# Larger base blocks on VectorE for the triangular inverse of a gated-delta chunk, with their operations preferred

## The chip, the cores and the metric

The kernel runs on one core of one Trainium2 chip. The metric is the device time of one execution in microseconds; for the kernel before it is the median of three runs. The profile shows one execution of the same program, taken by the hardware profiler; its times are in us from the start of the span. Engines are TensorE (PE; PEld are its weight loads), VectorE (DVE), ScalarE (ACT), GpSimd (POOL) and SyncE (SP).

## What is computed

One inference step of a two-layer decoder for 256 prompt tokens and 8 sample tokens that share the weights. Each layer adds a mixer (four mLSTM heads and eight gated-delta heads fed by one input projection), a cross-attention and a SwiGLU block to the residual; a final norm follows. What matters here is the gated-delta rule of a prompt, shown without batch and heads, for one chunk with keys k, decays g (cumulated) and step sizes beta:

```
decay_ts = exp(g_t - g_s)  for s <= t
A        = strictly_lower(decay_ts * (k @ k.T) * beta_s)
rhs      = v - exp(g) * (k @ S)
U        = triangular_solve(I + A, rhs)          # unit lower triangular
wu       = beta * U
o        = exp(g) * (q @ S) + (q @ k.T * decay_ts) @ wu
S        = exp(g_last) * S + (exp(g_last - g) * k).T @ wu
```

The keys and queries are normalised first, which needs the sum of squares of each row. The reference cuts the 256 tokens into chunks of 64, the kernel into two chunks of 128; the result is the same sum.

## The kernel before, in words

**Streams.** Nearly all time goes into products with weights. `stream` (with `block`) brings a weight block of 512 KB by DMA on SyncE's queue, splits it into a rounded part on ScalarE (`wh`, line 55) and the rest on VectorE (`wl`, line 61), and multiplies: per block 24 matmuls of 264 columns, three for each product (tile `acc`). One stream of 256 output features over 2048 inputs is 96 matmuls. The splits and what takes the accumulators out of PSUM stand under `tc.high_priority(offset=PRIO)` with PRIO = 1000.

**TensorE's order is written out by hand; the others' is planned.** The whole program stands under a manual schedule for TensorE: its instructions run in the order in which the Python code issues them. The other engines' instructions are ordered by a planner that runs before the launch: of the instructions that are ready in its own timeline it prefers those that were issued earlier, and `high_priority(offset=n)` counts an instruction as issued n earlier.

**Chains between the streams.** Everything beside the streams is a Python generator (a chain). `mm` and `tr` advance a clock by each matmul's columns / 2.4; a chain yields a number of these units, and `pump`, called after every few stream matmuls, resumes the chains whose time has come. So `yield 13000.0` puts the next matmuls of a chain that much further back in TensorE's order, to give the other engines time. If they aren't done by then, TensorE stands. `finish` runs chains that have to be over before an output projection.

**The mixer's order in a layer.** Four pairs of gated-delta heads, g = 0 to 3: for each, the streams of q, k and v (`gdn_inputs`, with the convolutions on VectorE), then two chains are spawned, `gdn_prompt` and `gdn_sample`; the stream of the gate z of the pair before comes next. Then the mLSTM streams and chains. A pair's `gdn_prompt` starts only when the one before has formed its last state (`R.formed`).

**`gdn_prompt`, step by step** (two heads and two chunks give four 128x128 matrices, side by side in tiles of 4x128 columns):
1. TensorE transposes the keys (tile kT) and ScalarE sums their squares (line 640); VectorE scales (`kss`, `rk`, `bs`, `kw`).
2. TensorE forms the products of keys (kk); VectorE makes N of them (line 58), which is A scaled.
3. `base_blocks` inverts the diagonal blocks of BASE = 8. ScalarE gathers the 32x32 diagonal blocks into tile u; VectorE transposes (lines 612, 617, 620) and runs a back substitution column by column, two operations for each column k (a product into scratch space of tile Dt, a subtraction in u); ScalarE copies the result into Dm. Dt is the transpose of Dm.
4. Meanwhile TensorE transposes values, queries (qT, with squares on ScalarE, line 671) and N (NT, copied to A).
5. After the long pause of line 680 come the doublings, for b = 8, 16, 32, 64: a product with A (pp), on VectorE a masked copy (Pf), a product with Dt (pd), on VectorE a subtraction in Dm and a transpose (line 715). Each turns inverses of b-blocks into inverses of 2b-blocks.
6. The solution, the outputs and the states of both chunks (pu, pS, pr), and the squares of the outputs (line 772).

`gdn_sample` does the same rule for the eight sample tokens (dks, then `rank1` with the matmuls dS that update the states on VectorE). The mLSTM chains (mqk, mvT, mkT, mn, mC) use the same four PSUM buffers (tag "m") as all chains.

**Scratch for squares.** `M.junk` hands out a tile of 128x256 with one buffer (`bufs=1`) for the unused elementwise result of a sum of squares; each call is a new tile in the same buffer.

Of the kernel before, what the change touches and what calls it, by code (L numbers as in the profile page):

```python
# [27 lines left out]
MEM = 256  # L28
EPS = 1e-6
WB, VB, SB, NV = 10, 6, 7, 6  # L30
BASE = 8
PRIO = 1000
Q0, K0, V0, O0 = 0, 512, 1024, 2048
IF0 = 3072
GQ0, GK0, GV0, GZ0 = 3080, 4104, 5128, 6152
# [13 lines left out]
def kernel(ctx: ExitStack, tc: tile.TileContext, io: dict, outs: list):  # L49
# [10 lines left out]
    def tt(out, a, b, op, eng=None):  # L60
        (eng or dve).tensor_tensor(out=out, in0=a, in1=b, op=op)  # L61
# [6 lines left out]
    def mm(out, lhsT, rhs, start=True, stop=True):  # L68
        n = 1
        for x in rhs.shape[1:]:  # L70
            n *= x
        clock[0] += max(n, lhsT.shape[-1]) / 2.4 * (1 if rhs.dtype == F32R else 4)
        pe.matmul(out=out, lhsT=lhsT, rhs=rhs, start=start, stop=stop)  # L73
# [37 lines left out]
    def ps(name):  # L111
        return pm.tile([P, 512], F32, name=name, tag="m")
# [429 lines left out]
    class Mix:  # L542

        def __init__(self, mx):

            self.mx, self.sampling = mx, False

        def w(self, name, shape=(4, P)):
            return self.mx.tile([P] + list(shape), F32, name=name, tag="w", bufs=WB)

# [17 lines left out]
            return self.mx.tile([P] + list(shape), F32, name=name, tag=name, bufs=2)  # L568

        def junk(self, p=P):  # L570
            return self.mx.tile([P, DV], F32, name="junk", tag="junk", bufs=1)[:p]

    def four(t):
        return t.rearrange("p (i t) -> p i t", i=4)
# [47 lines left out]
    def gdn_prompt(l, g, s, G, M, R):  # L622
# [12 lines left out]
        pkn = ps("kT")  # L635
        for i in range(4):
            tr(pkn[:, i * P:(i + 1) * P], ch(k, i))
        kss, rk, bs, kd = M.c("kss"), M.c("rk"), M.c("bs"), M.c("kd")
        for i in range(4):
            act.activation(M.junk()[:, :P], pkn[:, i * P:(i + 1) * P], AF.Square, accum_out=kss[:, i:i + 1])  # L640
        kw = M.w("kw")
        tt(kw, four(pkn), bc(E[:, :, P - 1], 2, P), ALU.mult)
        dve.tensor_scalar(out=kss, in0=kss, scalar1=4.0 * EPS, scalar2=None, op0=ALU.add)
        dve.reciprocal(out=rk, in_=kss)
        tt(bs.rearrange("p (h c) -> p h c", c=2), rk.rearrange("p (h c) -> p h c", c=2), bcol, ALU.mult)
        dve.tensor_scalar(out=kd, in0=kss, scalar1=0.25, scalar2=None, op0=ALU.mult)
        power(kd, hp)

        pk_ = ps("kk")
        for i in range(4):  # L650
            mm(pk_[:, i * P:(i + 1) * P], ch(k, i), ch(k, i))
        N = M.w("N")
        for i in range(4):
            stt(N[:, i], pk_[:, i * P:(i + 1) * P], bs[:, i:i + 1], E[:, i], ALU.mult, ALU.mult)

        Dm, Dt = M.w("Dm"), M.w("Dt")
        pool.memset(Dm, 0.0)
        base_blocks(N, Dm, Dt, M.v("u", (2, P)))
        yield 4500.0
        pv = ps("vT")  # L660
        for i in range(4):
# [6 lines left out]
            tr(pqn[:, i * P:(i + 1) * P], ch(q, i))  # L668
        qd = M.c("qd")
        for i in range(4):  # L670
            act.activation(M.junk()[:, :P], pqn[:, i * P:(i + 1) * P], AF.Square, accum_out=qd[:, i:i + 1])
        dve.tensor_scalar(out=qd, in0=qd, scalar1=4.0 * EPS, scalar2=float(DK), op0=ALU.add, op1=ALU.mult)
        power(qd, hm)
        A = M.w("A")
# [2 lines left out]
        for i in range(4):  # L677
            tr(pa[:, i * P:(i + 1) * P], N[:, i])
        copy(A, four(pa))
        yield 13000.0  # L680
        b = BASE
        while b < P:
            def halves(t, which, i=None):
# [85 lines left out]
        R.formed = True  # L769
        oss = M.c("oss")  # L770
        for i in range(4):
            act.activation(M.junk()[:, :P], o[:, i], AF.Square, scale=qd[:, i:i + 1], accum_out=oss[:, i:i + 1])
# [15 lines left out]
    def gdn_sample(l, g, s, G, M, R, S, smp):  # L788

        h0 = 2 * g  # L790
        kv, k3, r3, kqf = smp[:4]
        while M.sampling:
            yield 500.0
        M.sampling = True
        for kind, at in ((1, 0), (0, 32), (2, 64)):
            pool.tensor_copy(out=kv[:, :, at:at + NB], in_=s[kind][:, :, T:C])
            if kind < 2:
                pool.tensor_copy(out=kqf[:, :, at:at + 41 * 7 + 1:41], in_=s[kind][:, :, T:C])
        if not G.ready:
            while not G.ready:  # L800
                yield 500.0
            yield 8000.0
        yield 10500.0
        pks = ps("dks")
        for j in range(2):
            tr(pks[:, T + j * P:T + (j + 1) * P], kv[:, j])
        for j in range(2):
            for b in range(NB):
                mm(pks[:40, j * P:(j + 1) * P], kqf[:, j, b * 40:(b + 1) * 40], S[:, j, b], b == 0, b == NB - 1)
        kn, qn, vN = M.n("dkn"), M.n("dqn"), M.n("dvn")  # L810
        for i, (d, f) in enumerate(((kn, 1.0), (qn, 1.0), (vN, 0.5))):
            copy(d, pks[32 * i:32 * i + NB, T:].rearrange("p (h t) -> p h t", h=2), scale=f)
        qk = M.c("dqk", (2, 2))[:NB]
        c = M.c("dc", (2,))[:NB]
        for j in range(2):
            act.activation(M.junk(NB)[:, :P], kn[:, j], AF.Square, accum_out=qk[:, 0, j:j + 1])
            act.activation(M.junk(NB)[:, :P], qn[:, j], AF.Square, accum_out=qk[:, 1, j:j + 1])
# [12 lines left out]
        tt(c, c, bk, ALU.mult)  # L830
        oN = qn
        for j in range(2):
            stt(vN[:, j], pks[:NB, j * P:(j + 1) * P], a1[:, j:j + 1], vN[:, j], ALU.mult, ALU.add)
            dve.tensor_scalar(out=oN[:, j], in0=pks[32:32 + NB, j * P:(j + 1) * P], scalar1=er[:, j:j + 1],
                              scalar2=None, op0=ALU.mult)
            stt(oN[:, j], vN[:, j], c[:, j:j + 1], oN[:, j], ALU.mult, ALU.add)
        tt(kn, kn, bc(bk, 2, P), ALU.mult)
        three(k3, kn, False)
        three(r3[:, :, :P], vN, True)
        yield 12000.0  # L840
        ev = G.gs[:, h0 * NB:(h0 + 2) * NB].rearrange("p (h b) -> p h b", h=2)
        for j in range(2):
            yield from rank1(S[:, j], k3[:, j], r3[:, j], ev[:, j], M.mx, P)
            nc.sync.dma_start(out=s_S[l, :, h0 + j].rearrange("b k v -> k b v"), in_=S[:, j])
        M.sampling = False
        q = M.c("dq", (2,))[:NB]
        for j in range(2):
            act.activation(M.junk(NB)[:, :P], oN[:, j], AF.Square, accum_out=q[:, j:j + 1])
        dve.tensor_scalar(out=q, in0=q, scalar1=1.0 / DK, scalar2=EPS, op0=ALU.mult, op1=ALU.add)
        power(q, hm)  # L850
        tt(oN, oN, bc(q, 2, P), ALU.mult)
        yield 2500.0
        while R.z is None:
            yield 500.0
        pb = ps("db")
        for j in range(2):
            tr(pb[:, j * NB:(j + 1) * NB], oN[:, j], NB)
        x = M.c("dx", (2, NB))
        tt(x, pb[:, :2 * NB].rearrange("p (h b) -> p h b", h=2), R.z[:, :, T:C], ALU.mult)
        for j in range(2):  # L860
            split_gain(R.hh[:, R.at + j, T:C], R.hl[:, R.at + j, T:C], x[:, j], g_gain(l, h0 + j))
# [52 lines left out]
    def mlstm_prompt(l, h, q, k, v, G, M, R, ncol):  # L914
# [39 lines left out]
        dve.reciprocal(out=rd, in_=rd)  # L954
        for c in range(2):
            dve.tensor_scalar(out=hn[:, c], in0=pn[c][:, :DV], scalar1=rd[:, c:c + 1], scalar2=None, op0=ALU.mult)
            act.activation(M.junk(), hn[:, c], AF.Square, accum_out=hss[:, c:c + 1])
# [15 lines left out]
    def mlstm_sample(l, g, q, k, vs, G, M, R, Cs, smp):  # L973
# [63 lines left out]
        three(r3, vN, True)  # L1037
        s2 = M.c("sss", (2,))[:NB]
        for j in range(2):
            act.activation(M.junk(NB), hN[:, j], AF.Square, accum_out=s2[:, j:j + 1])  # L1040
# [527 lines left out]
```

## Time and profile before

| | |
|---|---|
| median of 3 runs | 2974.95 us (2973.18 to 2977.75) |
| the profiled execution | 2973.59 us |
| its span, first to last instruction | 2971.8 us |
| busy: TensorE, VectorE, ScalarE, GpSimd | 98%, 67%, 50%, 17% of the span |
| granted TensorE clock, mean over the span | 0.995 |
| VectorE busy from 80 to 120 us | 36.06 us of 40 |
| VectorE busy from 700 to 1600 us (layer 0's SwiGLU block) | 557.58 us of 900 |

A line such as "L73 PE MATMUL pp<-Dm,A 128*128 128x64 f32" names the line of the kernel (often that of a helper), the engine, the operation, the tile written and the tiles read by the program's names, and the shape. In a timeline a start and a duration stand ahead of it, and in brackets behind it the idle time of the engine just before, with what ended it. A row of a view by stretches gives the stretch, its length, each engine's busy time with its number of instructions (TensorE, weight loads, VectorE, ScalarE, GpSimd), the granted clock, the share of the DMA engines and GB/s. A row for a tile gives shortest, median and longest duration in ns, and the first and last start.

### The profile page before, as it was taken

To read this page: it belongs to the slowest core of one execution; us is meant where nothing else is said; L and a number is where in the kernel's file an instruction comes from. 1 tells how busy PE (TensorE), PEld (TensorE's weight loads), DVE (VectorE), ACT (ScalarE), POOL (GpSimd) and SP (SyncE) were. 2 spreads that over 40 slices of the span, in tenths; PEclk is the share of its full clock that TensorE was granted. 3 is DMA by queue.
4 is the path that set the end of the run, shared out by engine and by line. 5 is a ranking of instruction groups with operands and counts; after the bars stand their busy time and mean duration, and the time that the engine had idled before them with its cause. 6 is when DMAs were issued, how large, how long until landed. Compare 5 with 4: busy or idle time off the path is not lost.

```text
span 2971.8 us, 57750 instructions
## 1 busy us (share of the span) xinstructions
PE 2905.8 (98%) x23219; PEld 2829.3 (95%) x23219; DVE 2001.9 (67%) x3443; ACT 1486.3 (50%) x2505; POOL 503.5 (17%) x662
## 2 busy tenths in 40 slices
PE   8989999999999999999999999999999999999998
PEld 7989999978999999999999899999699999999998
DVE  7978776877555555555688877678765555555555
ACT  6656555666433343333466655556654333343435
POOL 5222100352100000000142211104520000001001
PEclk9999999999999999999999999999999999999999
DMA  7655565666666666666665564757756666666664
GB/s 193 167 147 157 152 199 161 214 212 190 183 179 180 182 179 182 179 181 180 181 182 153 151 181 120 215 153 222 231 171 179 183 179 181 181 180 183 178 183 130
DMA packets 381252, 530.08 MB, mean 178 GB/s; under 512 B 25576, under 2 KB 226224, under 8 KB 380960
## 3 DMA queue, kind: packets, MB, share of 16 engines
q1 hardware_dynamic: 364328, 498.74, 57.0%
q0 software_dynamic: 7424, 25.20, 2.8%
q10 hardware_dynamic: 9232, 2.45, 0.4%
q8 instruction: 182, 2.98, 0.4%
q14 instruction: 86, 0.70, 0.1%
HBM read 502.88 MB, written 23.83 MB: 177 GB/s over the span
## 4 chain that ended last, share of the span: by engine, by line
PE 88%; DVE 6%; ACT 3%; issue 2%; DMA 1%; POOL 0%; SPq 0%; POOLq 0%; ACTq 0%; DVEq 0%
PE acc L73 77%; PE kv L73 2%; DVE wl L61 2%; DVE xl L58 1%; PE dks L73 1%; ACT wh L55 1%; PE pp L73 1%; PE pd L73 1%; DMA memn<-in_mem_prompt_dram 1%; PE dS L73 1%; DVE xT L61 0%; PE sqC L73 0%; DVE p L1363 0%; PE accg L73 0%; PE so L73 0%
## 5 line engine op out<-in xcount | busy, mean ns | idle before, releaser
L61 DVE TENSOR_TENSOR wl<-raw,wh 128x1024 fp32r<-128x1024 f32 x880 | 1092.6, 1242 | 812.1 <-ACT wh L55 810.2
L55 ACT ACTIVATE wh<-raw 128x1024 fp32r<-128x1024 f32 x880 | 930.9, 1058 | 1200.3 <-PE acc L73 1079.2
L73 PE MATMUL acc<-xh,wh 128*128 128x264 f32 x4736 | 1367.2, 289 | 6.3 <-ACT wh L55 3.5
L73 PE MATMUL acc<-xl,wh 128*128 128x264 f32 x4736 | 1349.9, 285 | 1.6 <-DVE xl L58 1.6
L73 PE MATMUL acc<-xh,wl 128*128 128x264 f32 x4736 | 1350.3, 285 | 0.5 <-DVE wl L61 0.5
L73 PEld LDWEIGHTS acc<-xh,wh 128*128 128x128 f32 x4736 | 897.1, 189 | 11.4 <-issue 5.1
L73 PEld LDWEIGHTS acc<-xl,wh 128*128 128x128 f32 x4736 | 897.8, 190 | 4.6 <-DVE xl L58 2.3
L73 PEld LDWEIGHTS acc<-xh,wl 128*128 128x128 f32 x4736 | 896.0, 189 | 1.5 <-DVE wl L61 1.4
L73 PE MATMUL acc<-ffh,wh 128*128 128x264 f32 x1408 | 400.7, 285 | 0.6 <-DVE xT L61 0.5
L73 PE MATMUL acc<-ffl,wh 128*128 128x264 f32 x1408 | 400.8, 285 | 0.0
L73 PE MATMUL acc<-ffh,wl 128*128 128x264 f32 x1408 | 400.3, 284 | 0.0
L61 POOL TENSOR_TENSOR fg<-fg,rstd 128x264 f32<-128x264 f32 x88 | 94.3, 1101 | 1306.1 <-ACT fg L1450 1286.4
L73 PEld LDWEIGHTS acc<-ffh,wh 128*128 128x128 f32 x1408 | 264.8, 188 | 1.0 <-issue 1.0
L73 PEld LDWEIGHTS acc<-ffl,wh 128*128 128x128 f32 x1408 | 265.3, 188 | 0.0
L73 PEld LDWEIGHTS acc<-ffh,wl 128*128 128x128 f32 x1408 | 265.0, 188 | 0.0
L61 DVE TENSOR_TENSOR xT<-acc,xT 128x264 f32<-128x264 f32 x512 | 190.0, 422 | 17.6 <-PE acc L73 17.0
L61 POOL TENSOR_TENSOR sa<-sa,sq 128x264 f32<-128x264 f32 x96 | 95.7, 1015 | 177.7 <-ACT sq L317 177.4
L58 DVE SCALAR_TENSOR_TENSOR xl<-xT,cst,xh 128x264 fp32r<-128x264 f32 x96 | 78.7, 857 | 0.0
L55 ACT ACTIVATE wm<-r,msk 72x128 fp32r<-72x128 f32 (+1 forms) x192 | 68.6, 425 | 18.5 <-PE dS L73 14.1
L58 DVE SCALAR_TENSOR_TENSOR y<-y,cst,y 128x255 f32<-128x255 f32 (+1 forms) x144 | 64.1, 473 | 0.8 <-ACT y L55 0.4
L55 ACT ACTIVATE xh<-xT,cst 128x264 fp32r<-128x264 f32 x80 | 39.6, 507 | 29.3 <-DVE xT L61 29.3
L61 POOL TENSOR_TENSOR vl<-vc,vh 128x512 fp32r<-128x512 f32 x32 | 44.3, 1411 | 25.7 <-ACT vh L55 25.7
(516 smaller groups left out, 3326.1 us busy)
## 6 DMA issues: line engine op xcount, KB each, us to landing
raw<-in_w_in_dram SPq DMA_DIRECT2D x224, 512.0 KB
raw<-in_ffn_w_gate_dram SPq DMA_DIRECT2D x176, 512.0 KB
raw<-in_ffn_w_up_dram SPq DMA_DIRECT2D x176, 512.0 KB
raw<-in_ffn_w_down_dram SPq DMA_DIRECT2D x176, 512.0 KB
raw<-in_w_out_dram SPq DMA_DIRECT2D x64, 512.0 KB
S<-in_state_gdn_S_dram POOLq DMA_DIRECT2D x16, 512.0 KB, 7.3
out_dram<-S SPq DMA_DIRECT2D x16, 512.0 KB
Ct<-in_state_mlstm_C_dram POOLq DMA_DIRECT2D x8, 1024.0 KB, 6.6
```

Of the source, the lines that this page charges most:

```text
L55: act.activation(out, in_, AF.Copy, scale=scale)
L58: dve.scalar_tensor_tensor(out=out, in0=a, scalar=s, in1=b, op0=o0, op1=o1)
L61: (eng or dve).tensor_tensor(out=out, in0=a, in1=b, op=op)
L73: pe.matmul(out=out, lhsT=lhsT, rhs=rhs, start=start, stop=stop)
```

## The change

BASE becomes 16: `base_blocks` inverts 16x16 blocks, with 15 columns instead of 7, and the doublings begin at b = 16, so that one of the four stages is left out. The pause ahead of the doublings grows from 13000 to 19000. From the squares of the keys to the end of `base_blocks` everything stands under `high_priority(offset=AHEAD)` with AHEAD = 600. The scratch tile for squares is made once per layer, and calls for 128 columns use its two halves in turn.

```
-BASE = 8
-PRIO = 1000
+BASE = 16
+PRIO, AHEAD = 1000, 600
...
+            self.junks, self.turn = mx.tile([P, DV], F32, name="junk", tag="junk"), 0
...
         def junk(self, p=P):
-            return self.mx.tile([P, DV], F32, name="junk", tag="junk", bufs=1)[:p]
+            self.turn = 1 - self.turn
+            return self.junks[:p], self.junks[:p, self.turn * P:(self.turn + 1) * P]
...
-        kss, rk, bs, kd = M.c("kss"), M.c("rk"), M.c("bs"), M.c("kd")
-        for i in range(4):
-            act.activation(M.junk()[:, :P], pkn[:, i * P:(i + 1) * P], AF.Square, accum_out=kss[:, i:i + 1])
...
-        Dm, Dt = M.w("Dm"), M.w("Dt")
-        pool.memset(Dm, 0.0)
-        base_blocks(N, Dm, Dt, M.v("u", (2, P)))
+        with tc.high_priority(offset=AHEAD):
+            kss, rk, bs, kd = M.c("kss"), M.c("rk"), M.c("bs"), M.c("kd")
+            for i in range(4):
+                act.activation(M.junk()[1], pkn[:, i * P:(i + 1) * P], AF.Square, accum_out=kss[:, i:i + 1])
...
+            Dm, Dt = M.w("Dm"), M.w("Dt")
+            pool.memset(Dm, 0.0)
+            base_blocks(N, Dm, Dt, M.v("u", (2, P)))
         yield 4500.0
...
         copy(A, four(pa))
-        yield 13000.0
+        yield 19000.0
```

All other sums of squares take `M.junk(...)[1]` (128 columns) or `[0]` (256 columns) instead of a new tile.

More of the change, by code (lines that the diff above doesn't have):

```diff
@@ L637, in gdn_prompt @@
             tr(pkn[:, i * P:(i + 1) * P], ch(k, i))
-        kss, rk, bs, kd = M.c("kss"), M.c("rk"), M.c("bs"), M.c("kd")
-        for i in range(4):
[L640 to L654, printed above, removed]
-        Dm, Dt = M.w("Dm"), M.w("Dt")
-        pool.memset(Dm, 0.0)
-        base_blocks(N, Dm, Dt, M.v("u", (2, P)))
+        with tc.high_priority(offset=AHEAD):
+            kss, rk, bs, kd = M.c("kss"), M.c("rk"), M.c("bs"), M.c("kd")
+            for i in range(4):
+                act.activation(M.junk()[1], pkn[:, i * P:(i + 1) * P], AF.Square, accum_out=kss[:, i:i + 1])
+            kw = M.w("kw")
+            tt(kw, four(pkn), bc(E[:, :, P - 1], 2, P), ALU.mult)
+            dve.tensor_scalar(out=kss, in0=kss, scalar1=4.0 * EPS, scalar2=None, op0=ALU.add)
+            dve.reciprocal(out=rk, in_=kss)
+            tt(bs.rearrange("p (h c) -> p h c", c=2), rk.rearrange("p (h c) -> p h c", c=2), bcol, ALU.mult)
+            dve.tensor_scalar(out=kd, in0=kss, scalar1=0.25, scalar2=None, op0=ALU.mult)
+            power(kd, hp)
+            pk_ = ps("kk")
+            for i in range(4):
+                mm(pk_[:, i * P:(i + 1) * P], ch(k, i), ch(k, i))
+            N = M.w("N")
+            for i in range(4):
+                stt(N[:, i], pk_[:, i * P:(i + 1) * P], bs[:, i:i + 1], E[:, i], ALU.mult, ALU.mult)
+            Dm, Dt = M.w("Dm"), M.w("Dt")
+            pool.memset(Dm, 0.0)
+            base_blocks(N, Dm, Dt, M.v("u", (2, P)))
         yield 4500.0
@@ L670, in gdn_prompt @@
         for i in range(4):
-            act.activation(M.junk()[:, :P], pqn[:, i * P:(i + 1) * P], AF.Square, accum_out=qd[:, i:i + 1])
+            act.activation(M.junk()[1], pqn[:, i * P:(i + 1) * P], AF.Square, accum_out=qd[:, i:i + 1])
         dve.tensor_scalar(out=qd, in0=qd, scalar1=4.0 * EPS, scalar2=float(DK), op0=ALU.add, op1=ALU.mult)
@@ L771, in gdn_prompt @@
         for i in range(4):
-            act.activation(M.junk()[:, :P], o[:, i], AF.Square, scale=qd[:, i:i + 1], accum_out=oss[:, i:i + 1])
+            act.activation(M.junk()[1], o[:, i], AF.Square, scale=qd[:, i:i + 1], accum_out=oss[:, i:i + 1])
         dve.tensor_scalar(out=oss, in0=oss, scalar1=1.0 / DK, scalar2=EPS, op0=ALU.mult, op1=ALU.add)
@@ L815, in gdn_sample @@
         for j in range(2):
-            act.activation(M.junk(NB)[:, :P], kn[:, j], AF.Square, accum_out=qk[:, 0, j:j + 1])
-            act.activation(M.junk(NB)[:, :P], qn[:, j], AF.Square, accum_out=qk[:, 1, j:j + 1])
+            act.activation(M.junk(NB)[1], kn[:, j], AF.Square, accum_out=qk[:, 0, j:j + 1])
+            act.activation(M.junk(NB)[1], qn[:, j], AF.Square, accum_out=qk[:, 1, j:j + 1])
         dve.tensor_scalar(out=qk, in0=qk, scalar1=4.0 * EPS, scalar2=None, op0=ALU.add)
@@ L847, in gdn_sample @@
         for j in range(2):
-            act.activation(M.junk(NB)[:, :P], oN[:, j], AF.Square, accum_out=q[:, j:j + 1])
+            act.activation(M.junk(NB)[1], oN[:, j], AF.Square, accum_out=q[:, j:j + 1])
         dve.tensor_scalar(out=q, in0=q, scalar1=1.0 / DK, scalar2=EPS, op0=ALU.mult, op1=ALU.add)
@@ L956, in mlstm_prompt @@
             dve.tensor_scalar(out=hn[:, c], in0=pn[c][:, :DV], scalar1=rd[:, c:c + 1], scalar2=None, op0=ALU.mult)
-            act.activation(M.junk(), hn[:, c], AF.Square, accum_out=hss[:, c:c + 1])
+            act.activation(M.junk()[0], hn[:, c], AF.Square, accum_out=hss[:, c:c + 1])
         dve.tensor_scalar(out=hss, in0=hss, scalar1=1.0 / DV, scalar2=EPS, op0=ALU.mult, op1=ALU.add)
@@ L1039, in mlstm_sample @@
         for j in range(2):
-            act.activation(M.junk(NB), hN[:, j], AF.Square, accum_out=s2[:, j:j + 1])
+            act.activation(M.junk(NB)[0], hN[:, j], AF.Square, accum_out=s2[:, j:j + 1])
         dve.tensor_scalar(out=s2, in0=s2, scalar1=1.0 / DV, scalar2=EPS, op0=ALU.mult, op1=ALU.add)
```

## The prediction

> **What bounds the kernel now.** I read the page's first and fourth parts, then TensorE's waits, then the chain of waits and the timelines around the largest of them.
>
> ```profile
> PE 2905.8 (98%) x23219; PEld 2829.3 (95%) x23219; DVE 2001.9 (67%) x3443; ACT 1486.3 (50%) x2505; POOL 503.5 (17%) x662
> ...
> PE 88%; DVE 6%; ACT 3%; issue 2%; DMA 1%; POOL 0%; SPq 0%; POOLq 0%; ACTq 0%; DVEq 0%
> ```
>
> TensorE sets the end: 98% busy, 88% of the chain that ended last. So a change pays if it takes matmuls away, or takes waits out of TensorE's order, which is written out by hand; work on VectorE costs nothing as long as TensorE doesn't come to wait for it. What TensorE waits for (columns: us in total, times, longest), without the rows of stages that the change leaves alone:
>
> ```profile
> PE pp L73 <- issue: 9.5, 2, 4.8
> ...
> PE dS L73 <- ACT junk L671: 3.4, 2, 1.7
> PE kk L73 <- DVE dqn L834: 3.4, 2, 1.7
> ...
> PE mkT L77 <- DVE N L58: 2.4, 2, 1.2
> ...
> PE mvT L77 <- DVE kw L61: 1.6, 2, 0.8
> PE NT L77 <- DVE N L58: 1.5, 3, 0.6
> ```
>
> All six lie in the inverse's chain or beside it, once per layer (NT three times). The largest, on layer 0's second pair of heads (I call the four pairs g0 to g3), in the chain of waits and then on VectorE and ScalarE:
>
> ```profile
> 193.86 5.10 PE acc L73 x42
> ...
> 203.26 4.75 issue
> 208.01 1.94 PE pp L73 x8
> 209.95 2.57 PE acc L73 x12
> ```
>
> ```profile
> 206.30 0.31 DVE L617 STREAM_TRANSPOSE u<-u 128x128 f32<-128x128 f32 x1
> ...
> 207.94 0.71 DVE L620 STREAM_TRANSPOSE Dt<-Dm 128x512 f32<-128x512 f32 x1 [1.33 <-ACT Dm L55]
> ```
>
> TensorE reached the first doubling's matmuls (pp) at 203.26, but the 8x8 blocks left VectorE only at 206.6 (L617), and their copies and transpose (L620) came after that, 2.1 us later: the "issue" is a wait for VectorE. How much of VectorE these blocks get is the question of this change. Two answers for the four base_blocks stretches of layer 0 (first transpose to the end of L617): all work first, then the instructions of tile u alone (the blocks):
>
> ```profile
> 101.20:116.20 15.00, 15.00 (x127) 14.64 (x127) 14.88 (x40) 9.88 (x26) 7.17 (x12) 1.00 0.63 177
> 187.40:206.60 19.20, 15.86 (x128) 15.41 (x126) 19.00 (x52) 10.04 (x17) 2.37 (x5) 0.97 0.76 215
> ```
>
> ```profile
> 101.20:116.20 15.00, 4.66 (x18) 0.00 (x0) 0.00 (x0) 1.00 0.63 177
> 187.40:206.60 19.20, 4.71 (x18) 0.00 (x0) 0.00 (x0) 0.97 0.76 215
> 269.60:278.40 8.80, 4.65 (x18) 0.00 (x0) 0.00 (x0) 1.00 0.28 89
> 335.30:344.60 9.30, 4.76 (x18) 0.00 (x0) 0.00 (x0) 0.83 0.21 70
> ```
>
> VectorE (third pair of columns) is full in g0 and g1, 14.88 of 15.00 and 19.00 of 19.20 us. The blocks cost 4.7 us each time, and got a share of 4.66/15.00 = 0.31, 0.245, 0.53 and 0.51.
>
> **The change part by part.** *Removed: the doubling from 8.* One instance on TensorE:
>
> ```profile
> 124.25 1.00 PE L73 MATMUL pp<-Dm,A 128*128 128x64 f32 x8
> 125.06 0.37 PE L73 MATMUL acc<-xh,wh 128*128 128x264 f32 x1
> ...
> 127.54 1.00 PE L73 MATMUL pd<-Pf,Dt 128*128 128x64 f32 x8
> 128.35 0.37 PE L73 MATMUL acc<-xh,wh 128*128 128x264 f32 x1
> ```
>
> From the first pp to the next matmul 0.81 us, from the first pd 0.81. Four pairs in two layers make eight chains: 8 x 1.62 = **-13.0 us**, all on the bounding engine, with nothing that could hide it. Two PSUM tiles per chain go too. On VectorE the masked copy, the subtraction and a transpose go, 0.42 + 0.41 + 0.70 = 1.53 us per chain:
>
> ```profile
> L61 DVE TENSOR_TENSOR Pf<-pp,up x16: 400/420/425, 126.7 to 1835.8; 128x256 f32<-128x256 f32 x16
> L61 DVE TENSOR_TENSOR Dm<-Dm,pd x40: 267/406/422, 128.6 to 1851.9; 128x256 f32<-128x256 f32 x16, 32x128 f32<-32x128 f32 x16, 64x256 f32<-64x256 f32 x8
> L715 DVE STREAM_TRANSPOSE Dt<-Dm x16: 693/702/712, 129.0 to 1838.9; 128x512 f32<-128x512 f32 x16
> ```
>
> *Added: the larger blocks.* base_blocks does two operations per column k, of 128/BASE x k elements: 14 of 16k elements before, 30 of 8k after. Their cost by size in g0, and the transposes:
>
> ```profile
> 103.08 0.27 DVE L61 TENSOR_TENSOR Dt<-u,Dt 128x112 f32<-128x112 f32 x1
> ...
> 114.77 0.18 DVE L61 TENSOR_TENSOR Dt<-u,Dt 128x16 f32<-128x16 f32 x1
> ```
>
> ```profile
> L612 DVE STREAM_TRANSPOSE Dt<-u x24: 300/570/579, 101.2 to 1806.9; 128x384 f32<-128x384 f32 x16, 128x128 f32<-128x128 f32 x8
> ```
>
> The first two rows make a line: 0.165 us plus 0.94 ns an element. The mean size is 64 elements before (16 x 4) and after (8 x 8), so each stays at 0.225 us; 30 cost 6.75 us. Five transposes of 384 columns at 0.57 (before two, and a short one at 0.30) and L617's 0.31 make 3.16: **9.9 us a chain**, against 4.7. With the 1.53 removed VectorE gets 3.7 more per chain, 29 us in all; it lies beside matmuls, and its price is only what TensorE waits at pp.
>
> *Moved: when TensorE comes for the blocks.* The pause ahead of the doublings grows from 13000 to 19000 units of the program's own matmul clock, which counts 264/2.4 = 110 for a matmul that took 5.10/42 = 0.1216 us: pp comes 6.6 us later. Due times: g0 124.25 + 6.6 = 130.9, g1 203.26 + 6.6 = 209.9, and from the first starts of pp in g2 and g3
>
> ```profile
> L73 PE MATMUL pp<-Dm,A x8: 218/275/275, 286.1 to 286.8; 128*128 128x64 f32 x8
> ```
>
> ```profile
> L73 PE MATMUL pp<-Dm,A x8: 275/275/323, 363.2 to 364.0; 128*128 128x64 f32 x8
> ```
>
> 292.7 and 369.8. A chain is 6 longer and a stage of 2100 + 1900 shorter, so each next pair starts some 2 us later in the streams; nothing waits for the last one's end.
>
> Are the blocks ready by then? At the shares of before, with 2.1 us for copies and transpose: g0 101.2 + 9.9/0.31 + 2.1 = 135.2, late; g1 187.4 + 9.9/0.245 + 2.1 = 229.9, very late; g2 269.6 + 9.9/0.53 + 2.1 = 290.4 and g3 335.3 + 9.9/0.51 + 2.1 = 356.8, in time. Once TensorE stands, no stream feeds VectorE and the rest runs nearly alone, so a wait is shorter than the lateness: in g0 29.7 x 0.31 = 9.2 us are done at the due time, and 0.7 + 2.1 = 2.8 are left; in g1 5.5 are done, 4.4 + 2.1 = 6.5 left, where 4.75 was the wait before.
>
> *Preferred: everything from the squares to the blocks*, as if written 600 instructions earlier. The weights' splits keep their 1000 and stay ahead:
>
> ```profile
> L61 DVE TENSOR_TENSOR wl<-raw,wh 128x1024 fp32r<-128x1024 f32 x880 | 1092.6, 1242 | 812.1 <-ACT wh L55 810.2
> ```
>
> One of 1.24 us for every 24 matmuls (2.92 us) takes 43%, which bounds the blocks' share at 0.57 from above; from below the old shares bound it, since the blocks were already written ahead of much that ran between their steps. I take the middle between 0.53 (VectorE with little else) and the old shares: 0.42 in g0, 0.39 in g1. g0 is then ready at 101.2 + 23.6 + 2.1 = 126.9, in time. g1 also starts earlier. Its squares on ScalarE, in the chain of waits:
>
> ```profile
> 170.78 0.50 ACT junk L772 x2
> ...
> 173.63 1.85 ACT wm L55 x6
> ...
> 178.73 0.36 ACT junk L640 x2
> ```
>
> All squares wrote one scratch tile, so those of k (L640) had to follow those of o (L772), and let other work in between, to 179.1. In two halves, and preferred, they can run from 173 to 175: 4 us earlier. Ready at 183.4 + 25.4 + 2.1 = 210.9 against 209.9: no margin at all. I take half of the old wait: **-4.7** of 9.5 us (from -9.5 to 2 x 1.75 = +3.5). The scratch tile itself costs nothing: the same ScalarE instructions. The preferred part issues no DMA; on GpSimd it puts a power of 128x4, a memset and a copy ahead, and GpSimd is busy for 17% of the span.
>
> *The clock.* TensorE's granted clock (third column from the end) fell behind these waits; I show the first, second and last of five such stretches:
>
> ```profile
> 181.40:184.80 3.40, 3.40 (x18) 3.40 (x17) 2.60 (x13) 1.35 (x7) 2.70 (x4) 0.50 0.58 167
> 205.30:212.10 6.80, 4.09 (x19) 4.12 (x20) 2.31 (x8) 1.23 (x4) 0.00 (x0) 0.50 0.74 224
> ...
> 1799.30:1802.70 3.40, 3.17 (x15) 3.17 (x16) 3.18 (x10) 2.02 (x4) 0.53 (x2) 0.51 0.02 5
> ```
>
> ```profile
> 181.23 3.72 PE acc L73 x18
> ```
>
> Behind 203.26, pp took 1.94 for 0.81 and twelve matmuls 2.57 for 12 x 0.1216: 2.2 us lost; at 181.4, eighteen took 3.72 for 2.19: 1.5 lost. g1 of layer 1 I count at 1.5 too. Half of g1's go with half of its wait, **-1.9**; the one at 181.4 hangs on the dS wait and goes, **-1.5**.
>
> The Trainium skill, "TensorE: Matmul & The Clock Gate", section "HAM oscillation", asks for no idle gap over some 3.4 us. By that rule the dS wait of 1.7 us would cost no clock, and the sum would be 1.5 us less of a gain; the row at 181.4 speaks against it.
>
> *The other waits.* NT waits for N, which is preferred now: **-1.5** (0 to -1.5). dS waits for squares of q, which follow those of k: **-2.5** of 3.4 (0 to -3.4). kk waits for a sample operation (dqn) that now stands behind preferred ones, but comes later: 0 (-3.4 to +3.4). mkT and mvT wait for g3's N and kw, sooner done but moved on into the mLSTM's use of the same four PSUM tiles: 0 (-4.0 to +4.0). What is late next is what the blocks pass: convolutions of the next pair and the state updates that free dS: **+3**, between 0 and the added 5.2 us once a layer, 10.4.
>
> **Sum:** -13.0 - 4.7 - 1.9 - 1.5 - 1.5 - 2.5 + 3 = -22.1 on the profiled execution's 2973.6 us (span 2971.8 and 1.8 around it): 2951.5. The median of the runs is 1.4 above that execution: **2953**.
>
> **The rivals.** *All in time.* The preference gets the blocks 0.5 everywhere; pp, NT, dS and kk waits go with their clock: -13.0 - 9.5 - 3.7 - 1.5 - 1.5 - 3.4 - 3.4 = -36.0, with the median's 1.4 **2939**. For it: g2 and g3 had that share. Against: 14.88 of 15.00.
>
> *The preference changes no order* (the change doesn't do what it says). For it: the blocks' operations were written before the convolutions that ran between them, and 0.31 was all they got; only their dependence on each other can explain that. Then g0 waits 2.8 + 1.5 of clock, g1 1.75 more, in both layers 12.1, against -13.0: **2974**.
>
> *VectorE has no room: slower.* The 9.9 us meet as many other operations in every pair, and the share falls to 0.3 or below in g2 as well. At 0.3: g0 1.0 + 2.1 + 1.5 = 4.6, g1 5.25 - 4.75 = 0.5, g2 23.1 x 0.3 = 6.9 done, 3.0 + 2.1 + 1.5 = 6.6; 11.7 a layer, 23.4 - 13.0 = +10.4: **2985**. It decides once new waits pass 6.5 us a layer. For it: 19.00 of 19.20; against: g2 needs only 9.9/(292.7 - 269.6 - 2.1) = 0.47, and had 0.53.
>
> **How the numbers follow.** The forecast gets 0.42, with 2943 to 2964 of its own; all in time 0.22; no order changed 0.18; no room 0.18. Faster or slower means over 0.2% (6 us), about what the runs can tell from none. Faster: 0.42 + 0.22 + 0.02 of the third; same 0.15; slower 0.18 + 0.01. The range reaches from below all in time, 2932, to 2978, and leaves out a twentieth below and the larger part of no room above.
>
> **What would show it.** 128x64 pp rows halved, and TensorE's busy time down by some 13 us: the sure step. "pp" gone from TensorE's waits: all in time; there with some 2 us per layer: the forecast; 3 us ahead of the first pp in g0: no order changed; pp waits in g2: no room. Block instructions' share of VectorE near 0.4 in the first two pairs; squares of k ended 2 us behind those of o; fewer than five half-clock stretches. Wrong in kind would be a longer wait of dS, acc or mqk in these stretches: then the blocks' preference is paid by whom they pass.

## The result, and the profile after

The changed kernel takes **2994.76 us** (median of three runs, 2990.93 to 2995.57) against 2974.95 before: a ratio of **1.0063**, 95% interval 1.0049 to 1.0077. It is slower by 19.8 us; the forecast was 2953, and the range ended at 2978.

The page of the changed kernel, its busy times and its chain of waits:

```profile
PE 2901.5 (97%) x23091; PEld 2825.9 (94%) x23091; DVE 2019.8 (67%) x3562; ACT 1479.6 (49%) x2505; POOL 507.1 (17%) x660
...
PE 84%; DVE 9%; ACT 2%; DMA 2%; issue 2%; POOL 1%; SPq 0%; POOLq 0%; ACTq 0%; DVEq 0%
```

The span of the profiled execution is 2993.0 us, 21.2 more than before. TensorE has 128 matmuls less but its busy time fell by 4.3 us only, and its time without work grew from 2971.8 - 2905.8 = 66.0 to 2993.0 - 2901.5 = 91.5 us, by 25.5. VectorE's part of the chain rose from 6% to 9%. What TensorE waits for (us in total, times, longest), without most rows of stages that the change leaves alone:

```profile
PE pp L73 <- ACT Dm L55: 38.3, 6, 9.8
...
PE ssq L73 <- POOL sa L61: 5.0, 2, 2.5
...
PE sqC L73 <- DVE sl L61: 4.0, 2, 2.0
...
PE mkT L77 <- DVE N L58: 3.6, 2, 1.8
...
PE NT L77 <- DVE N L58: 1.9, 2, 1.0
PE kk L73 <- DVE dqn L838: 1.5, 2, 0.8
...
PE mvT L77 <- DVE kw L61: 1.5, 2, 0.7
...
PE dS L73 <- DVE kw L61: 0.2, 1, 0.2
```

The waits of pp for the finished blocks went from 9.5 us (one per layer) to 38.3 (three per layer: 3.60, 9.81 and 5.76 us in layer 0). In g0 and g2 pp starts 1.4 us after the last block instruction; in g1 it starts 3.2 us after it, since ScalarE had eight instructions for wm ahead of its copies into Dm, so some 1.8 of the 9.81 us are ScalarE's. The dS wait of 3.4 is down to 0.2 and kk's from 3.4 to 1.5. The blocks' stretches on layer 0, g0 to g3 (first transpose to the end of the last block instruction but one, now L620), all work first and then, for g0, tile u alone:

```profile
100.29:132.05 31.76, 29.60 (x245) 29.02 (x243) 31.13 (x87) 20.65 (x52) 8.80 (x15) 1.00 0.53 150
190.13:222.70 32.57, 25.98 (x212) 25.16 (x210) 29.56 (x90) 15.62 (x38) 3.79 (x8) 0.94 0.66 194
276.44:304.30 27.86, 23.48 (x193) 22.69 (x191) 25.43 (x79) 17.41 (x48) 7.91 (x8) 1.00 0.49 138
348.02:382.10 34.08, 32.06 (x248) 30.99 (x248) 32.91 (x102) 23.30 (x51) 6.58 (x13) 1.00 0.39 117
```

```profile
100.29:132.05 31.76, 9.34 (x36) 0.00 (x0) 0.00 (x0) 1.00 0.53 150
```

The reader is to see three things. The blocks' own work is 9.34 us (9.34 to 9.40 in the others). The stretches are 28 to 34 us long, against 9 to 19 before, so the blocks' share of VectorE is 0.27 to 0.34 everywhere. And beside the 36 block instructions VectorE ran 87 - 36 = 51, 54, 43 and 66 others (in the first three, one of them had started before). A piece of its timeline in g0 (start, duration, operation) shows how they lie:

```profile
102.13 0.28 DVE L61 TENSOR_TENSOR Dt<-u,Dt 128x120 f32<-128x120 f32 x1
102.33 0.48 DVE L58 SCALAR_TENSOR_TENSOR y<-y,cst,y 128x254 f32<-128x254 f32 x1
102.72 1.22 DVE L61 TENSOR_TENSOR wl<-raw,wh 128x1024 fp32r<-128x1024 f32 x1
103.85 0.48 DVE L58 SCALAR_TENSOR_TENSOR y<-y,cst,y 128x254 f32<-128x254 f32 x1
104.25 0.28 DVE L61 TENSOR_TENSOR u<-u,Dt 128x120 f32<-128x120 f32 x1
```

Column 15's product is done at 102.41, and the subtraction that needs it starts at 104.25, behind two convolution operations and a split. This is VectorE's order as the planner wrote it, in spite of the preference.

The other loss is the clock. These are the first and the last of seven stretches at half clock in the changed kernel, six of them behind pp waits, and the sum of all seven:

```profile
133.70:140.50 6.80, 6.80 (x33) 6.70 (x32) 3.13 (x7) 2.34 (x5) 0.00 (x0) 0.50 0.11 39
...
2086.10:2089.50 3.40, 3.40 (x18) 3.40 (x17) 1.69 (x3) 3.39 (x6) 0.00 (x0) 0.51 0.37 132
sum 58.10, PE 40.22 PEld 39.87 DVE 29.67 ACT 30.89 POOL 4.55; mean PE 5.75 PEld 5.70 DVE 4.24 ACT 4.41 POOL 0.65
```

TensorE was busy for 40.2 us at half clock, against 17.4 in the five stretches before. There the stream's matmuls start 0.220 us apart, for 0.1216 at full clock, so 0.45 of the difference, some 10 us, is time lost to the clock. The busy time's -4.3 is then +10 of clock and some -14.5 for the rest, of which the prediction had -13.0 for the stage left out.

### The profile page after: what moved, and what is told of

Read it like the earlier page. It is cut to its first block, busy times and chain, and to the rows that moved or that the text cites. A ratio compares the mean times of both kernels' runs of the same rounds, so it can differ in the third digit from the quotient of the medians.

```text
span 2993.0 us, 57591 instructions
## 1 busy us (share of the span) xinstructions
PE 2901.5 (97%) x23091; PEld 2825.9 (94%) x23091; DVE 2019.8 (67%) x3562; ACT 1479.6 (49%) x2505; POOL 507.1 (17%) x660
## 4 chain that ended last, share of the span: by engine, by line
PE 84%; DVE 9%; ACT 2%; DMA 2%; issue 2%; POOL 1%; SPq 0%; POOLq 0%; ACTq 0%; DVEq 0%
PE acc L73 75%; DVE wl L61 2%; DVE xl L58 1%; PE kv L73 1%; PE dks L73 1%; PE pp L73 1%; DVE xT L61 1%; ACT wh L55 1%; PE pd L73 1%; PE dS L73 1%; PE sqC L73 0%; DMA raw<-in_w_in_dram 0%; DMA memn<-in_mem_prompt_dram 0%; DVE p L1367 0%; PE accg L73 0%
## 5 line engine op out<-in xcount | busy, mean ns | idle before, releaser
L73 PE MATMUL pp<-Dm,A 32*32 32x32 f32 (+2 forms) x256 | 22.5, 249 | 38.3 <-ACT Dm L55 38.3
L73 PEld LDWEIGHTS pp<-Dm,A 32*32 32x32 f32 (+2 forms) x256 | 19.4, 159 | 41.9 <-ACT Dm L55 32.0
```

## The experiments

The theory I began with (T1 in the expectations): the whole loss is the blocks' lateness at pp, since each dependent block operation has other work ahead of it whatever is preferred; VectorE has the time for them. Medians stand beside runs of the kernel before on the same chip (2974.07 to 2975.91 us in the four groups); "ratio" is to these.

### The preference alone

```
-        with tc.high_priority(offset=AHEAD):
+        if True:
```

> The changed kernel without the preference; 16x16 blocks, the pause and the two halves of the scratch tile stay. Theory T1 (the loss is the blocks' own lateness at pp: 35 dependent VectorE steps in place of 17, each with other operations between it and the next, and the preference does not change that order): no different from the changed kernel within 4 us, that is 2991 to 2999 us, with the pp waits of layer 0 still near 3.6, 9.8 and 5.8 us. Rival T2 (the preference itself does the harm, by pushing other operations back): 2989 us or less.

Measured: 2993.36 us, ratio 1.0063 (1.0048 to 1.0078). Its first wait:

```profile
PE pp L73 <- ACT Dm L55: 38.3, 6, 9.8
```

The row is the same to the tenth, and so is the whole order: in the two profiles VectorE's 3562 instructions, ScalarE's 2505 and GpSimd's 660 follow each other in the same order with and without the preference. It does no harm (T2 falls) and no good. Most of what runs between the blocks' steps was issued behind them already: when such work is held back (below), the others between the first and the last of them in g0 fall from 50 to 8. My reading, which this run doesn't show by itself, is that what keeps a step back is that it isn't ready when the planner fills the place behind the step before.

### The two halves, with blocks of 8

Against the changed kernel (as all diffs here, but where a line says so):

```
-BASE = 16
+BASE = 8
...
-        yield 19000.0
+        yield 13000.0
```

> Blocks of 8 and the old pause of 13000 come back; the preference and the two halves stay. T1: these two parts hardly move anything: 2970 to 2977 us, the pp wait of the second pair of heads (4.75 us before) shorter by no more than the 2 us by which the blocks' front came earlier. T2: slower than before by 6 us or more, 2981 us up.

Measured: **2963.39 us**, ratio 0.9962 (0.9948 to 0.9976): 11.5 us faster than before, where neither theory had more than 5. Without the preference this program, too, has the same order, so the gain is that of the two halves. Its waits:

```profile
PE pp L73 <- issue: 12.0, 2, 6.0
...
PE kk L73 <- DVE dqn L838: 2.0, 2, 1.0
```

pp waits 2.5 us more, but dS (3.4 before) and NT are gone from the list, and kk waits less; TensorE's time without work is 2961.6 - 2902.7 = 58.9 us against 66.0. ScalarE shows the reason best in the squares of q, of the kernel before and then of the changed one (the reading of a square's sum, and the next square):

```profile
179.28 0.19 ACT L671 ACTIVATION_READ_ACCUMULATOR junk<-qT 128x1 f32 x1
179.51 0.28 ACT L671 ACTIVATE junk<-qT 128x128 f32<-128x128 f32 x1
```

```profile
183.33 0.20 ACT L675 ACTIVATION_READ_ACCUMULATOR junk<-qT 128x1 f32 x1
183.43 0.28 ACT L675 ACTIVATE junk<-qT 128x128 f32<-128x128 f32 x1
```

With one tile a square starts when the reading of the sum before has ended (179.28 + 0.19 = 179.47), 0.40 us after the last square's start; with two halves ahead of that end (183.53), 0.25 us after it. A square that writes the same scratch as its predecessor has to follow it; one that writes the other half need not. The edit also makes the tile once per layer instead of once per square, but that isn't what helps: the two squares of line 1044, which each write the whole of the tile made once, still start 0.52 us apart and behind the reading, as before. Nor do all squares gain: those of the outputs (line 776) run chunk by chunk, i = 0 and 2 first, so that neighbours get the same half, and stay 0.53 us apart; with columns of their own (last experiment) it is 0.39. That the planner then also places squares earlier among other work I take from the waits that went; it isn't shown by itself.

### One scratch tile in the changed kernel

```
         def junk(self, p=P):
-            self.turn = 1 - self.turn
-            return self.junks[:p], self.junks[:p, self.turn * P:(self.turn + 1) * P]
+            t = self.mx.tile([P, DV], F32, name="junk", tag="junk", bufs=1)
+            return t[:p], t[:p, :P]
```

> The changed kernel with one scratch tile for all squares, as before the change, in place of the two halves. With blocks of 8 the two halves were worth 11.5 us. If they are worth as much here, 3001 to 3010 us. If they work by the sample's squares and the blocks' front alone, which now end far from pp, no difference within 4 us: 2989 to 2999.

Measured: 3004.40 us, ratio 1.0100 (1.0084 to 1.0115): 9.6 us above the changed kernel. The halves are worth about as much with either size of block.

```profile
PE dS L73 <- ACT wm L55: 6.5, 2, 3.2
...
PE kk L73 <- ACT eL L593: 3.4, 2, 1.7
```

With one tile these two waits for ScalarE are there again (1.7 us of kk, as before the change), but pp waits 6.5 us less, and TensorE's time without work is 3004.2 - 2912.0 = 92.2 us, hardly more than 91.5. What grew is its busy time, by 10.5 us: it was busy for 62.8 us at half clock in ten stretches, in place of 40.2 in seven. So here the halves pay by the clock, while with blocks of 8 most of the gain was in the waits.

### The old pause with blocks of 16

```
-        yield 19000.0
+        yield 13000.0
```

(and no preference)

> Blocks of 16 and the two halves, no preference, with the old pause of 13000: what the longer pause of the change is worth. 42, 49, 23 and 27 others stand between the block instructions of a pair in place of 47, 42, 37 and 63. T1: pp comes 6.6 us earlier and the blocks in the first two pairs hardly do: waits of some 8, 14 and 5 us per layer in the first three pairs, 3000 to 3020 us. If it is the longer pause that harms: 2985 us or less.

Measured: 3014.66 us, ratio 1.0133 (1.0118 to 1.0148), as T1 has it, though pp now waits in all four pairs.

```profile
PE pp L73 <- issue: 40.1, 6, 11.1
PE pp L73 <- ACT Dm L55: 9.8, 2, 5.1
```

With these the change can be put together: the halves -11.5, the preference 0, blocks of 16 at the old pause +51.3 (2963.39 to 3014.66), the longer pause -21.3 (to 2993.36); together +18.5, the difference of the kernel without preference to the one before.

### A longer pause still

```
-        yield 19000.0
+        yield 21000.0
```

> The changed kernel with the pause ahead of the doublings at 21000 in the place of 19000, about 2.2 us of TensorE's time more per pair of heads. T1: each of the six pp waits shrinks by about 2.2 us (3.6, 9.8, 5.8 to about 1.4, 7.6, 3.6), 13 us in all, and up to 6 us of clock with them: 2975 to 2983 us. T3: no change within 5 us, 2990 to 3000.

Measured: 2986.30 us, ratio 1.0040 (1.0025 to 1.0055), a gain of 7 to 8 us where T1 had 12 to 20.

```profile
PE pp L73 <- issue: 14.9, 4, 4.5
PE pp L73 <- ACT Dm L55: 9.9, 2, 4.9
...
PE dS L73 <- DVE kw L61: 5.6, 2, 2.8
...
PE sqC L73 <- ACT sh L55: 3.1, 2, 1.5
PE mC L73 <- DVE kw L61: 3.0, 2, 1.5
```

The pp waits shrank as expected, by 38.3 - 24.8 = 13.5 us. But rows of dS, sqC and mC with 11.7 us came in: a pair's chain that ends later meets the next pair and the mLSTM streams. The pause isn't free.

### Nobody waits for the blocks

```
-    mm(ppi[:, i], A[:, i], halves(Dm, 1, i))
+    mm(ppi[:, i], A[:, i], halves(kw, 1, i))
...
-    mm(pdi[:, i], Dt[:, i], f[:, i])
+    mm(pdi[:, i], kw[:, i], f[:, i])
```

(and the same for the stages of 32 and 64). First with blocks of 16 and the pause of 19000:

> The changed kernel, but TensorE's products of the doublings read the tile kw in the place of Dm and Dt; they are as many and as large, VectorE does all that it did, and only the wait of TensorE for the blocks is gone (the inverse that comes out is another one). T1: the 38.3 us of pp waits go, and of the 40.2 us that TensorE was busy at half clock most, a gain of up to 18 us more: 2935 to 2948 us. Rival T3 (it is the 29 us of added VectorE work that delays evictions and with them other stages, whoever waits for the blocks): 2965 us or more, the waits turning up at other rows.

Measured: 2956.51 us, ratio 0.9941 (0.9926 to 0.9955). 38 us go with the wait, which is most of what T1 had; but 9 to 21 us of it stay away, so T3 isn't without ground either. The same edit with blocks of 8 and 13000:

> Blocks of 8, the old pause and the two halves (2963.4 us), with TensorE's products of the doublings reading the tile kw in the place of Dm and Dt: nothing of TensorE's work is left out, only the wait for the blocks (the inverse that comes out is another one). To be set beside the same edit with blocks of 16 (2956.5 us). Theory A (blocks of 16 lose by being late alone; in time they would win the 13 us of the stage): 2966 to 2972 us, that is 2956.5 + 13. Theory B (the added VectorE work costs about what the stage saves even where nothing waits for the blocks, as other stages then wait): 2942 to 2952 us, which is 2963.4 less the 12.0 us of pp waits and some 5 us of clock.

Measured: 2946.89 us, ratio 0.9908 (0.9893 to 0.9923): theory B. With this wait out of the way blocks of 16 are still 9.6 us slower than blocks of 8. To separate the pause from the blocks, blocks of 16 with 13000:

> Blocks of 16 whose result TensorE's doublings don't wait for (they read kw), as in the run of 2956.5 us, with the old pause of 13000, so that it differs from the same edit with blocks of 8 (2946.9 us) in the blocks alone. If the 9.6 us between those two come from the added VectorE work, they stay: 2952 to 2962 us. If they come from the longer pause, 2930 to 2945 us, since the stage of 13 us is then left to be won.

Measured: 2946.33 us, ratio 0.9903 (0.9888 to 0.9917), between the two expectations. The longer pause is what costs the 10 us. At the same pause blocks of 16 and of 8 are equal (2946.3 and 2946.9): TensorE is busy for 2886.4 us against 2897.9, 11.5 less for the stage left out, and without work for 2944.7 - 2886.4 = 58.3 us against 2945.2 - 2897.9 = 47.3, 11.0 more. New rows of the kernel with 16, among others:

```profile
PE dS L73 <- ACT wm L55: 6.4, 2, 3.2
...
PE pu L73 <- DVE Dm L61: 4.3, 2, 2.2
...
PE pd L73 <- DVE Dm L61: 2.2, 2, 1.1
```

Two of them name Dm, and so does one of mC (1.9 us). They may be the blocks' lateness again, at the place where the inverse is used at last, which this edit leaves in. So I don't call the 11 us shown to be VectorE's load alone; that stays open.

### Steps or work

```
                 tt(D[:, :, :k], D[:, :, :k], tmp[:, :, :k], ALU.subtract)
+                for _ in range(2):
+                    dve.tensor_scalar(out=D[:, :, k - 1], in0=D[:, :, k - 1], scalar1=1.0, scalar2=None, op0=ALU.mult)
```

(with blocks of 8, pause 13000, two halves, no preference)

> Blocks of 8, the old pause and the two halves (2963.4 us), with 14 very small dependent VectorE instructions added to each pair's blocks (two after each column, a factor of 1.0 on one column, about 0.15 us each, some 2 us per pair in all). Theory S (what lengthens the blocks is the number of dependent steps, each of which lets about as many other instructions through: some 41, 28, 37 and 25 stand between now in place of 18, 28, 9 and 14): the blocks take some 10 us longer in most pairs and pp waits in three of them, 2980 us or more. Theory W (it is the work that counts): 2 us per pair, 2963 to 2971 us.

Measured: 3010.48 us, ratio 1.0122 (1.0107 to 1.0137): **47 us slower** than the 2963.39 without these instructions. The stretches of g0 and g2 on VectorE, all instructions, then g0 with tile u alone, and TensorE's first waits:

```profile
102.36:128.18 25.82, 25.14 (x77) 1.00 0.52 144
...
275.75:299.75 24.00, 21.70 (x71) 1.00 0.52 140
```

```profile
102.36:128.18 25.82, 7.15 (x32) 0.00 (x0) 0.00 (x0) 1.00 0.52 144
```

```profile
PE pp L73 <- issue: 27.7, 4, 9.0
PE pp L73 <- ACT Dm L55: 14.1, 2, 7.1
```

Beside them g0 and g2 of the kernel of 2963.39 us, all instructions of VectorE:

```profile
102.33:117.29 14.96, 14.86 (x40) 1.00 0.62 177
...
265.32:276.93 11.61, 10.02 (x30) 1.00 0.49 138
```

The blocks' work grew by some 2.5 us (18 instructions took 4.7 us before the change), but the stretches by 10.9 and 12.4 us, and by 10.3 in g3, since 77 - 32 = 45 and 71 - 32 = 39 others stand between in place of 40 - 18 = 22 and 30 - 18 = 12. In g1, where 38 stood between, 38 do now, and the stretch grew by 3.1 us alone. Each dependent step lets 1.4 and 1.2 other instructions through here; in the kernel before it was 22/18 = 1.2 in g0, 34/18 = 1.9 in g1 and 8/18 = 0.4 in g2, in the changed one 51/36 = 1.4, 1.5, 1.2 and 1.8. Theory S holds in three pairs of four: **the block chain grows with its number of dependent steps, far beyond their own work**; in g0 each step costs (25.14 - 7.15)/32 = 0.56 us of other work, against the 0.22 that it takes itself. How many others a step lets through is no constant, though; it seems to depend on what is there to run.

### Holding other work back

```
+    def behind():
+        return tc.issue_after(tail[-1]) if tail else contextlib.nullcontext()
...
-        dve.transpose(Nc, u[:, 1])
+        tail.append(dve.transpose(Nc, u[:, 1]).ins)
...
-            for j in range(2):
-                ti = 8 * kind + h0 + j
...
+            with behind():
+                for j in range(2):
+                    ti = 8 * kind + h0 + j
```

`issue_after` puts what follows behind the named instruction in VectorE's order, without a wait of its own; `behind` stands ahead of the convolutions of a stream and ahead of the sample's step, both indented below it. The first kernel is the changed one with this; the second has a pause of 13000, the third blocks of 8 and 13000.

> The changed kernel, with the VectorE instructions of the convolutions and of the sample step held back, where they are written behind a pair's blocks, until the last block instruction but one has gone out. Nothing is added or left out; only VectorE's order changes: between the first and the last of the 36 block instructions of a pair stand 8, 15, 3 and 50 others in place of 47, 42, 37 and 63. Theory T1 (the blocks are late because other work stands between their dependent steps; VectorE has the time): the blocks end ahead of pp in the first three pairs, the 38.3 us of pp waits go and with them up to 18 us of clock: 2938 to 2960 us. Rival T4 (VectorE is full in these stretches, 31.8 of 33.8 us in the first, and what is held back is itself needed, so that other waits take the place): 2975 us or more.

> As the one before it, with the old pause of 13000, so that pp comes some 6.6 us earlier; 8, 12, 12 and 27 others stand between the block instructions. T1: the blocks are still in time or late by a few us at one pair: 2935 to 2960 us, and within 8 us of the one with 19000. T4: 2975 us or more.

> Blocks of 8, pause of 13000, the two halves, and the same holding back; 4, 16, 7 and 14 others stand between the 18 block instructions of a pair, in place of 18, 28, 9 and 14 (2963.4 us). T1: the two pp waits of 6.0 us shrink or go, and the two stretches of half clock with them: 2946 to 2958 us. And the stage that blocks of 16 leave out is worth what TensorE spends in it, 13 us: this kernel is 6 to 14 us slower than the one with blocks of 16 and 13000. T4: 2963 us or more, and blocks of 16 still the slower.

Measured: 3000.89 us (ratio 1.0084, 1.0067 to 1.0101) against 2994.76 without holding back; 3011.59 (1.0124, 1.0109 to 1.0139) against 3014.66, no certain difference; 2979.94 (1.0019, 1.0010 to 1.0029) against 2963.39. T1 is right on the cause of the pp waits and wrong on the time, which is T4's. TensorE's first waits in the first of them, GpSimd at the place of the longest, and all engines in the stretch ahead of it:

```profile
PE dks L78 <- POOL mvn L945: 26.7, 2, 13.3
PE dks L78 <- POOL kv L806: 17.4, 2, 8.7
```

```profile
286.53 0.20 POOL L806 COPY kv<-s 128x16 f32<-128x16 f32 x1 [14.37 <-DVE s L59]
```

```profile
273.40:286.78 13.38, 0.05 (x1) 0.00 (x0) 11.46 (x39) 1.87 (x5) 0.23 (x2) 0.61 0.14 39
```

No pp wait for the blocks is left; in g1 they took 23.3 us in place of 32.6, and in g2 12.5 in place of 27.9. So the order decides whether the blocks are late. But the convolutions behind them gave their result s late, GpSimd's copy of it into kv waited for 14.4 us, and TensorE's dks for the copy (the longer row names mvn, which GpSimd wrote 0.13 us later, but dks reads kv): 44.1 us of waits for 38.3. TensorE stood for these 13.38 us while VectorE was busy for 11.46 of them: what was held back was needed as soon as the blocks.

### A version that beats both

Two more edits on the two halves with blocks of 8. First the pause:

```
-        yield 13000.0
+        yield 14000.0
```

> Blocks of 8 and the two halves, no preference, and a pause of 14000 in place of 13000, so that pp comes 1.1 us later; 18, 16, 9 and 21 other VectorE instructions stand between the block instructions of a pair in place of 18, 28, 9 and 14. T1: the two pp waits of 6.0 us go and the clock with them: 2945 to 2955 us. If a longer pause brings other waits, as 21000 in the place of 19000 did with blocks of 16 (2.8 us of dS, 3.1 and 3.0 of other rows per two layers): 2958 us or more.

Measured: 2959.38 us, ratio 0.9949 (0.9933 to 0.9966), which can't be told from the 0.9962 with 13000 for certain. The pp waits of 6.0 us went, but a wait of NT for N, 3.2 us per layer, came in their place: three of the four squares of k in g1 came only from 176.3 on, and N with them. Then room for each group of squares, with 13000 and with 14000:

```
-    act.activation(M.junk()[1], pkn[:, i * P:(i + 1) * P], AF.Square, accum_out=kss[:, i:i + 1])
+    act.activation(Dm[:, i], pkn[:, i * P:(i + 1) * P], AF.Square, accum_out=kss[:, i:i + 1])
...
-    act.activation(M.junk()[1], pqn[:, i * P:(i + 1) * P], AF.Square, accum_out=qd[:, i:i + 1])
+    act.activation(A[:, i], pqn[:, i * P:(i + 1) * P], AF.Square, accum_out=qd[:, i:i + 1])
...
-    act.activation(M.junk()[1], o[:, i], AF.Square, scale=qd[:, i:i + 1], accum_out=oss[:, i:i + 1])
+    act.activation(W[:, i], o[:, i], AF.Square, scale=qd[:, i:i + 1], accum_out=oss[:, i:i + 1])
```

(The tiles Dm and A are made earlier for it.)

> Blocks of 8, pause of 13000; the three groups of four squares of a pair write their unused results each into a tile of the pair that is free at that time (Dm, A and W, four separate columns blocks), and only the sample's and the others' squares keep the two halves. If the halves helped because a square has to follow the one that wrote the same scratch before it, more room helps further: 2950 to 2961 us. If two are enough, no difference from 2963.4 within 4 us.

> The same with the pause of 14000 (2959.4 us with the two halves). If more room helps: 2945 to 2957 us; otherwise 2956 to 2963 us.

Measured: 2962.76 us (ratio 0.9958, 0.9941 to 0.9974) and **2948.54 us** (0.9908, 0.9894 to 0.9923). At 13000 it gives nothing: pp still waits for g1's blocks, 5.5 us per layer. At 14000 it gives 11 us; what is left of pp's waits for the blocks is

```profile
PE pp L73 <- ACT Dm L55: 6.0, 2, 3.0
```

and NT waits no more: in g1 the squares of k now follow each other without other work between from 169.24 on, the last of the four at

```profile
170.00 0.29 ACT L645 ACTIVATE Dm<-kT 128x128 f32<-128x128 f32 x1
```

This kernel is 27 us faster than the runs of the one before beside it and 46 faster than the changed one, with blocks of 8 and all matmuls left in.

## Why the prediction was wrong

**The stage left out, -13.0: right, and paid back.** The 128x64 products of pp were halved, and TensorE's busy time, freed of the clock, fell by some 14.5 us; between the two kernels that wait for no block, by 11.5.

**The cost of the larger blocks, 9.9 us a chain: right** (9.34 us in the rows above, without the last transpose). VectorE's whole busy time rose by 17.9 us, less than the 29 of the working. The 2.1 us behind the blocks were too much: pp reads Dm, not its transpose, and started 1.4 us after the blocks both before (206.61 to 208.01) and in g0 and g2 now.

**The step that failed: "I take the middle between 0.53 (VectorE with little else) and the old shares: 0.42 in g0, 0.39 in g1."** It rested on the preference. The preference changed no instruction's place, and the share came out at 9.34/31.76 = 0.29 in g0, also 0.29 in g1, 0.34 in g2 (it had been 0.53) and 0.27 in g3. In g0 that is below what I took as the lower bound, and g2 and g3, which I took to keep 0.53 and 0.51, fell furthest. I took the share as a property of the stretch, so that 9.9 us of work would take 9.9 over the share. The runs show a chain of 36 dependent steps with 1.2 to 1.8 other instructions in each gap; the share is what comes out of that. The stretch grew from 15.0 to 31.8 us in g0, from 19.2 to 32.6 in g1, from 8.8 to 27.9 in g2 and from 9.3 to 34.1 in g3.

For g0 the trace of before held what was needed, and so did the working, ahead of the preference: its old share gives 9.9/0.31 = 31.9 us (31.8 measured), and 36 steps with 22/18 others each give 44 others (51 measured). For g1 both say too much (40.4 us for 32.6), and for g2 both say too little: 18.7 us for 27.9, and 36 x 8/18 = 16 others for 43. The row of g2 before, all instructions, of which 18 are the blocks':

```profile
269.60:278.40 8.80, 8.80 (x75) 8.28 (x74) 7.92 (x26) 4.89 (x11) 1.28 (x2) 1.00 0.28 89
```

In the 19.6 us after it, to 298.0, VectorE ran 43 instructions and was busy for 17.05 us. A chain that is three times as long runs into such work; that this is where g2's further 35 others come from I infer from these two rows.

**pp 6.6 us later: right as a size.** g0's pp was due at 133.49 - 3.60 = 129.9 (130.9 in the working), and it bought what a pause can buy: 21.3 us against the same blocks at 13000. What the sum left out is its price. "Nothing waits for the last one's end" was wrong: where TensorE waits for no block, 19000 instead of 13000 costs 10.2 us, and 21000 brought waits of dS, sqC and mC.

**"The scratch tile itself costs nothing": wrong, to the good.** It was worth 11.5 us with blocks of 8 and 9.6 with 16, the only part of the change that gains. In g1 the k squares ended 9.2 us behind the transposes of the keys in place of 11.8, so 2.6 us of the 4 that I had counted on were there (the eight instructions for wm still stood ahead of them); the gain came at kk and dS, which I had put down to the preference, and with blocks of 16 mostly by the clock.

**The clock, -3.4: the sign was wrong.** With waits of 3.6 to 9.8 us in three pairs, some +10. The rule of the Trainium skill that I weighed ("TensorE: Matmul & The Clock Gate", section "HAM oscillation", no gap of over some 3.4 us) would have charged all three pairs' waits, which are longer than that; I believed those of g0 and g2 away and g1's halved. The trace agrees with it in these cases (half clock from 133.7, 219.0 and 304.4 on); the last section has waits where it doesn't.

**The other waits:** NT -1.5 (measured +0.4), dS -2.5 (-3.2), kk 0 (-1.9), mkT and mvT 0 (+1.1), and none of the +3 for work pushed back, as nothing was. A new one was sqC, +4.0.

**The rivals.** "The preference changes no order" had the mechanism, with its test: 3 us ahead of the first pp in g0 (3.60 measured). It kept the old shares, and so missed g2's wait of 5.76. "VectorE has no room" had the size of the share, 0.3 everywhere, a pp wait in g2 (5.1 us worked out, 5.76 measured), and the sign; 2985 was still 10 us too fast, as it counted g1 at 5.25 us for the 9.81 measured, and 1.5 us of clock for each wait. The two are one mechanism, and I had given them 0.36 together.

## What to carry to other kernels

Where a planner orders an engine ahead of time, a chain of dependent operations on a busy engine costs its own work and, for each step, what stands between two of them. Before trading a matmul stage on the bounding engine for twice as many dependent steps elsewhere, count the others per step and multiply; and look at what is there to run behind the old chain's end, since a longer chain runs into it. A preference can't help a step that isn't ready; look whether any instruction changes its place before counting on it. And a scratch tile that nobody reads still orders everybody who writes it: give writers that run next to each other their own room, it was the cheapest 10 us here.

## What the runs showed of the hardware that I had not expected

Waits shorter than 3.4 us can lose the clock. The stretches of half clock last 3.4 us or a multiple (6.8, 13.7), and they lie on one grid: three of the changed kernel begin at 133.7, 219.0 and 304.4, 85.3 = 25 x 3.41 us apart. Each begins at the end of a stretch of 3.4 us in which TensorE was busy for about half or less. For the first and the last of the changed kernel, whose rows stand above (133.70 and 2086.10), this is the stretch ahead; between them stands one on the same grid, with a wait of 2.0 us at sqC, that kept the full clock:

```profile
130.30:133.70 3.40, 0.21 (x2) 0.24 (x3) 2.00 (x5) 1.23 (x4) 0.00 (x0) 1.00 0.51 152
...
376.06:379.47 3.41, 1.63 (x14) 1.38 (x12) 3.41 (x12) 2.24 (x6) 0.00 (x0) 1.00 0.45 144
...
2082.70:2086.10 3.40, 1.46 (x10) 1.40 (x11) 1.29 (x1) 1.17 (x3) 1.81 (x2) 1.00 0.83 255
```

So 1.46 us of work in 3.40 lost the clock and 1.63 in 3.41 kept it. Before the change 1.68 in 3.40 (from 178.00) lost it, so no sharp threshold comes out of these rows. The last stretch holds a wait of 2.5 us at ssq. The layer before has the same wait and kept the full clock after it: there it fell on two stretches of the grid (from 604.75 and from 608.16), with 2.00 and 2.32 us of work. So a wait of some 2 us costs clock, or not, in part by where it falls. In the stretch from 2086.10 matmuls start 0.220 us apart for 0.1216, so that some 1.5 of its 3.40 us are lost. The Trainium skill ("TensorE: Matmul & The Clock Gate", section "HAM oscillation") speaks of gaps over some 3.4 us; by these rows 1.9 us without work in a stretch of 3.4 were enough.
